# Reciprocal roots of the Hyena filters: a ScalarE square root and one Newton step in place of a bit trick and three, and the skip weight added on GpSimd

## The chip, the cores and the metric

The kernel runs on one core of one Trainium2 chip. The metric is the device time of one execution in microseconds (us), median of several runs. The profile names the engines PE (TensorE matmul), PEld (TensorE weight load), DVE (VectorE), ACT (ScalarE), POOL (GpSimd) and SP (the queue that issues most DMAs).

## What is computed

A trunk of two layers over 1024 latent tokens of width 1024, with a 256-token context. Layer 0 is neighbourhood attention beside a bidirectional gated DeltaNet. Layer 1 is an order-2 Hyena: its long convolutions take filters that a small network generates. The change is in those filters, which depend on no token:

```python
def hyena_filters(length, w1, b1, f1, w2, b2, f2, w3):
    ...
    hid = jnp.sin(f1 * (feats @ w1 + b1))
    hid = jnp.sin(f2 * (hid @ w2 + b2))
    h = (hid @ w3).astype(jnp.float32).reshape(length, HY_ORDER, HY_DIRS, HY_W)
    decay = jnp.abs(jnp.linspace(HY_DECAY_MIN, HY_DECAY_MAX, HY_W, dtype=jnp.float32))
    h = h * jnp.exp(-t * decay)[:, None, None, :]
    return h * lax.rsqrt(jnp.sum(h * h, axis=0, keepdims=True) + EPS)

def long_conv(u, h_fwd, h_bwd, skip):
    ...
    return (y_f + y_b + u32 * skip.astype(jnp.float32)).astype(u.dtype)
```

There are 2 orders x 2 directions x 1024 channels of filters, each of 1024 points. The skip weight is added to point 0 of the even part of a filter pair before its transform, which gives the same result as the last line.

## The kernel before

The program is written engine by engine in no order of its own: a scheduler in the build, which works with its own estimate of times, puts the instructions of each engine into one fixed list, and each engine works through its list in that order, waiting on semaphores. A change of a few instructions can therefore move others.

`start()` is the first stage. It does three things side by side. For each of eight blocks `cb` of 128 channels, `filter_pair` makes four filters (`od` = 0 to 3; two orders, two directions): two matmuls per half (tile `fh`), a multiply by the decay `dec` on DVE (L1265), a square with a row sum on ACT (L1267, into `ss`). After each second filter it adds EPS on DVE (L1270), takes the reciprocal root of the two sums (`rsqrt`, tile `rr`), and scales the two filters on ACT (L1273). `filter_block` then forms their sum `pp` (tile `fp`) on POOL (L1287) and difference on DVE (L1288), adds the skip weight to column 0 of `pp` (L1289), folds both (L1120 to L1143, L1301) and transposes them on PE; `filter_spectrum` multiplies by DFT matrices on PE and combines the results on DVE (L1324 to L1327) into the tile `G`, which goes to HBM for layer 1. The steps are staggered by `flush`: the block of one pair is put out while the next pair is made.

Beside this, `start()` brings in the latent tokens (`load_x`, `layer0_in`, L378 to L398), computes the modulation vectors (`mod_block`, L204 to L227) and the gate path of layer 0 (`zblock`, whose Tanh on ACT is L481 and whose product on DVE is L482). After `start()` comes `project()`, where PE runs the projections of layer 0.

`rsqrt` (L76 to L96) takes a first guess from the bits of its argument (L82, L83) and makes three Newton steps; for the two columns of a filter pair that is 12 DVE instructions, each on a 128x2 tile and each reading the one before it:

```python
for c in (3.0, 12.0, 768.0):
    nc.vector.tensor_tensor(t, s, s, ALU.mult)
    nc.vector.tensor_tensor(t, t, y, ALU.mult)
    ...
```

It is called 16 times for filters (tiles `fr_i`, `fr_t`, result `frr`); its other calls, for tokens and heads, have other tile names and do not change.

Of the kernel before, what the change touches and what calls it, by code (L numbers as in the profile page):

```python
# [10 lines left out]
F32 = mybir.dt.float32  # L11
# [3 lines left out]
AF = mybir.ActivationFunctionType  # L15
ALU = mybir.AluOpType
# [45 lines left out]
class Kernel:  # L62
# [13 lines left out]
    def rsqrt(self, out, y, n, pool, tag):  # L76

        nc = self.nc
        shape = [out.shape[0], n]
        ti = pool.tile(shape, I32, name=tag + "_i", tag="rsq_i")  # L80
        t = pool.tile(shape, F32, name=tag + "_t", tag="rsq_t")
        nc.vector.tensor_scalar(ti, y.bitcast(I32), 1, None, ALU.logical_shift_right)  # L82
        nc.vector.tensor_scalar(ti, ti, -1.0, float(0x5F3759DF), ALU.mult, ALU.add)  # L83

        s = ti.bitcast(F32)
        for c in (3.0, 12.0, 768.0):
            if n == 1:
                nc.vector.scalar_tensor_tensor(t, s, s, y, ALU.mult, ALU.mult)
            else:
                nc.vector.tensor_tensor(t, s, s, ALU.mult)  # L90
                nc.vector.tensor_tensor(t, t, y, ALU.mult)
            if c < 768.0:
                nc.vector.scalar_tensor_tensor(s, t, -c, s, ALU.add, ALU.mult)
            else:
                nc.vector.tensor_scalar(t, t, -c, -1.0 / 8192.0, ALU.add, ALU.mult)
                nc.vector.tensor_tensor(out, s, t, ALU.mult)  # L96

    def split(self, src, hi, lo, lo_eng=None, hi_eng=None):

        nc = self.nc  # L100
        if hi_eng is None:
            nc.scalar.copy(hi, src)  # L102
        else:
            hi_eng.tensor_copy(hi, src)
        (lo_eng or nc.gpsimd).tensor_tensor(lo, src, hi.bitcast(F32), ALU.subtract)  # L105
# [1136 lines left out]
    def filter_pair(self, cb, w3, fil, pst, psp, psf, fw):  # L1242

        nc, ap, fa = self.nc, self.ap, self.fa
        hid, trow, ndel, skip, mats = fil

        ws = fa.tile([P, 4, P], F32R, name=f"w3s_{cb}", tag="w3s", bufs=2)
        nc.scalar.copy(ws, w3)
        nc.gpsimd.tensor_tensor(w3[FFN:], w3[FFN:], ws[FFN:].bitcast(F32), ALU.subtract)
        nc.scalar.copy(ws[FFN:], w3[FFN:])  # L1250
        dec = fa.tile([P, L], F32, name=f"dec{cb}", tag="dec", bufs=1)
        nc.scalar.activation(dec, trow, AF.Exp, scale=ndel[:, cb:cb + 1])
        hh, hl = hid
        for od in range(4):
            if od % 2 == 0:
                ss = self.small.tile([P, 2], F32, name=f"fss{cb}_{od}", tag="fss")
                rr = self.small.tile([P, 2], F32, name=f"frr{cb}_{od}", tag="frr")
                hs = []
            t = fa.tile([P, 1028], F32, name=f"fh{cb}_{od}", tag="fh", bufs=4)
            for q in range(2):  # L1260
                sl = slice(q * 512, (q + 1) * 512)
                ps = psp.tile([P, 512], F32, name=f"fh{cb}_{od}_{q}", tag="g")
                nc.tensor.matmul(ps, ws[:, od, :], hh[:, sl], start=True, stop=False)
                nc.tensor.matmul(ps, ws[:FFN, od, :], hl[:, sl], start=False, stop=True)
                nc.vector.tensor_tensor(t[:, sl], ps, dec[:, sl], ALU.mult)  # L1265
            junk = self.xp.tile([P, L], BF16, name=f"fjk{cb}_{od}", tag="junk", bufs=1)
            nc.scalar.activation(junk, t[:, :L], AF.Square, accum_out=ss[:, od % 2:od % 2 + 1])  # L1267
            hs.append(t)
            if od % 2:
                nc.vector.tensor_scalar_add(ss, ss, EPS)  # L1270
                self.rsqrt(rr, ss, 2, self.small, f"fr{cb}_{od}")
                for d in range(2):
                    nc.scalar.activation(hs[d][:, :L], hs[d][:, :L], AF.Copy, scale=rr[:, d:d + 1])  # L1273
                self.flush(0, lambda a=(cb, od // 2, hs, skip, mats, pst, psf, fw): self.filter_block(*a))
# [7 lines left out]
    def filter_block(self, cb, o, hs, skip, mats, pst, psf, fw):  # L1282
        nc = self.nc
        nm = f"{cb}_{o}"
        pp = fw.tile([P, 1028], F32, name="fp" + nm, tag="fp", bufs=2)
        hf, hb = hs
        nc.gpsimd.tensor_tensor(pp[:, :L], hf[:, :L], hb[:, :L], ALU.add)  # L1287
        nc.vector.tensor_tensor(hb[:, :L], hf[:, :L], hb[:, :L], ALU.subtract)  # L1288
        nc.vector.tensor_tensor(pp[:, 0:1], pp[:, 0:1], skip[:, o, cb:cb + 1], ALU.add)  # L1289
        nc.gpsimd.memset(pp[:, L:L + 1], 0.0)  # L1290
        v, g = nc.vector, nc.gpsimd
        xTs = [None, None]
        for side, u in ((1, hb), (0, pp)):

            f = fw.tile([P, 10, P], F32, name=f"ff{nm}_{side}", tag="ff", bufs=2)
            f4 = f[:, 0:8, :].rearrange("p (h b k) m -> p h b k m", h=2, b=2)
            s1, d1, d2 = self.fold_tree(u, fw, f"ft{nm}_{side}", (g, v)[side])
            self.fold(f4[:, ::-1 if side else 1, :, 1, :], u, 1024, v, side)
            self.fold(f4[:, 0, :, 0, :], d1, 512, v, side)
            self.fold(f[:, 4, :], d2, 256, v, side)  # L1300
            g.tensor_tensor(f[:, 6:9:2, :], s1[:, 0:256].rearrange("p (a b) -> p a b", b=P),  # L1301
                            s1[:, 256:512].rearrange("p (a b) -> p a b", b=P), ALU.add)
            xTs[side] = self.transpose_all(f.rearrange("p a b -> p (a b)"), 9, fw, pst, f"fx{nm}_{side}", "xT", 3)
        self.flush(1, lambda: self.filter_spectrum(cb, o, xTs, mats, psf, fw))
# [619 lines left out]
```

## Time and profile before

| | us |
|---|---|
| median of 3 runs | 1977.28 |
| lowest and highest of them | 1976.55 and 1983.64 |
| the profiled execution, its time | 1978.44 |
| the same, span from first to last instruction | 1976.7 |
| PE busy | 1758.5 (89%) |
| DVE busy | 1452.9 (74%) |
| ACT busy | 817.4 (41%) |
| POOL busy | 709.7 (36%) |

The profiled execution took 1.7 us more than its span. Busy shares are averages over stages with different limits: the stage that the change touches, `start()`, fills about the first fifth of the span, and what matters is what each engine does in that stretch. A group's mean duration on DVE and POOL includes time in which an instruction stood waiting while it was already started. Lines are those of the kernel before.

### The profile page before, as it was taken

The page shows a single profiled execution, that of the slowest core. Times are in us where ns is not written, and L with a number is a line of the kernel's source. Part 1 is how long each engine was busy: PE and PEld are TensorE (multiplying, and loading weights), DVE is VectorE, ACT ScalarE, POOL GpSimd, SP SyncE. Part 2 cuts the span into 40 slices and gives each one's busy share as a digit, 9 for nine tenths or more (in the row PEclk, how much of TensorE's full clock was granted, in tenths as well). Part 3 has the DMA queues.
Part 4 walks back from the last instruction along what each step waited for, and adds up shares of the span by engine and source line. Part 5 has one row for each costly group of instructions (what it writes and reads, how often), then busy time and mean ns, then how long its engine had stood idle before and what let it go on. Part 6 is the DMA issues. An engine that isn't in the chain of part 4 may idle for free. (4 is left out here: it accounts for less than half of the span.)

```text
span 1976.7 us, 30354 instructions
## 1 busy us (share of the span) xinstructions
PE 1758.5 (89%) x11156; PEld 1425.0 (72%) x11156; DVE 1452.9 (74%) x2786; ACT 817.4 (41%) x1811; POOL 709.7 (36%) x878
## 2 busy tenths in 40 slices
PE   7698997999988989999977899879889899999888
PEld 2365765688866778787756787768778788878776
DVE  5999899666746644646554566579989999999766
ACT  4555574354534424233343344524323423433421
POOL 0776455422566777411253202511121221221310
PEclk9797998999998999999988999989999999999989
DMA  7423255423343564644688733511221121222324
GB/s 279 160 84 114 83 188 173 141 71 109 123 141 108 182 193 149 199 155 153 160 203 202 190 126 124 166 55 45 66 78 55 55 91 61 80 66 78 113 95 144
DMA packets 127471, 250.07 MB, mean 127 GB/s; under 512 B 43433, under 2 KB 65465, under 8 KB 125274
## 3 DMA queue, kind: packets, MB, share of 16 engines
q1 hardware_dynamic: 123482, 233.45, 36.0%
q0 software_dynamic: 3840, 14.68, 3.8%
q8 instruction: 88, 1.44, 0.3%
q14 instruction: 61, 0.50, 0.1%
HBM read 172.06 MB, written 76.03 MB: 126 GB/s over the span
## 5 line engine op out<-in xcount | busy, mean ns | idle before, releaser
L647 DVE SCALAR_TENSOR_TENSOR dacc<-dpad,convw,dacc 128x1024 f32<-128x1024 f32 (+1 forms) x80 | 84.4, 1084 | 24.1 <-ACT dacc L645 20.1
L116 PE MATMUL hx<-h1h,w1x_hi 128*128 128x512 f32 x256 | 101.1, 395 | 0.0
L116 PE MATMUL hx<-h1l,w1x_hi 128*128 128x512 f32 x256 | 101.0, 394 | 0.0
L116 PE MATMUL hx<-h1h,w1x_lo 128*128 128x512 f32 x256 | 100.7, 393 | 0.0
L112 PE MATMUL dn<-hh,wdn_lo 128*128 128x512 f32 (+1 forms) x256 | 94.9, 372 | 5.8 <-POOL wdn_lo L105 5.8
L111 PE MATMUL dn<-hl,wdn_hi 128*128 128x512 f32 (+1 forms) x256 | 94.8, 370 | 0.0
L110 PE MATMUL dn<-hh,wdn_hi 128*128 128x512 f32 (+1 forms) x256 | 94.5, 369 | 0.0
L750 POOL TENSOR_TENSOR sub<-Lb,Xb 80x31 f32<-80x31 f32 (+15 forms) x124 | 78.7, 635 | 38.8 <-DMA Lb<-lsc_d 18.3
L752 POOL TENSOR_TENSOR Xb<-Xb,sub 80x31 f32<-80x31 f32 (+15 forms) x124 | 84.9, 684 | 8.4
L105 POOL TENSOR_TENSOR w1x_lo<-w1x_raw,w1x_hi 128x1024 fp32r<-128x1024 f32 x16 | 53.7, 3355 | 90.6 <-ACT w1x_hi L102 90.5
L1045 ACT ACTIVATE pr<-pr,st 128x640 f32<-128x640 f32 (+1 forms) x64 | 51.3, 802 | 69.1 <-DVE st L1044 68.5
L112 PEld LDWEIGHTS dn<-hh,wdn_lo 128*128 128x128 f32 x256 | 48.7, 190 | 14.5 <-POOL wdn_lo L105 6.1
L1287 POOL TENSOR_TENSOR fp<-fh,fh 128x1024 f32<-128x1024 f32 x16 | 41.2, 2577 | 41.5 <-ACT fh L1273 41.5
L121 PE MATMUL pt<-ident,pr 128*128 128x128 f32 x304 | 48.6, 289 | 8.3 <-ACT pts L1058 4.2
L1616 DVE SCALAR_TENSOR_TENSOR hu<-hpx,hyconv,hu 128x1024 f32<-128x1024 f32 x32 | 53.5, 1671 | 2.1 <-ACT hu L1614 2.0
L1154 ACT COPY fx<-fx_ps 128x512 f32<-128x512 f32 (+1 forms) x96 | 43.8, 483 | 27.0 <-PE fx_ps L121 26.6
L116 PEld LDWEIGHTS hx<-h1h,w1x_lo 128*128 128x128 f32 x256 | 48.1, 188 | 9.1
L116 PEld LDWEIGHTS hx<-h1l,w1x_hi 128*128 128x128 f32 x256 | 48.1, 188 | 8.9
L116 PEld LDWEIGHTS hx<-h1h,w1x_hi 128*128 128x128 f32 x256 | 48.1, 188 | 8.9
L111 PEld LDWEIGHTS dn<-hl,wdn_hi 128*128 128x128 f32 x256 | 48.7, 190 | 8.0 <-issue 0.5
L1267 ACT ACTIVATE fjk<-fh 128x1024 bf16<-128x1024 f32 x32 | 33.9, 1059 | 49.5 <-DVE fh L1265 40.7
L110 PEld LDWEIGHTS dn<-hh,wdn_hi 128*128 128x128 f32 x256 | 48.7, 190 | 7.7
(565 smaller groups left out, 6069.5 us busy)
## 6 DMA issues: line engine op xcount, KB each, us to landing
hG<-g_d SPq DMA_DIRECT2D x16, 1088.0 KB
g_d<-G SPq DMA_DIRECT2D x16, 1024.0 KB
em_w<-in_em_w SPq DMA_DIRECT2D x24, 512.0 KB
om_w<-in_om_w SPq DMA_DIRECT2D x24, 512.0 KB
wz_raw<-in_w0z SPq DMA_DIRECT2D x16, 512.0 KB
w1x_raw<-in_w SPq DMA_DIRECT2D x16, 512.0 KB
wdn_raw<-in_w0dn SPq DMA_DIRECT2D x12, 512.0 KB
wn_raw<-in_w0na SPq DMA_DIRECT2D x12, 512.0 KB
```

The source lines that it names most:

```text
L105: (lo_eng or nc.gpsimd).tensor_tensor(lo, src, hi.bitcast(F32), ALU.subtract)
L110: nc.tensor.matmul(ps, wh, xh, start=start, stop=False)
L111: nc.tensor.matmul(ps, wh, xl, start=False, stop=False)
L112: nc.tensor.matmul(ps, wl, xh, start=False, stop=stop)
L116: ins = self.nc.tensor.matmul(*args, **kw)
L121: ins = self.nc.tensor.transpose(out, x, self.ident)
L647: nc.vector.scalar_tensor_tensor(acc[:, t0:t0 + n], pad[:, o + j:o + j + n], cw[:, blk, j:j + 1], acc[:, t0:t0 + n], ALU.mult, ALU.add)
L750: nc.gpsimd.tensor_tensor(tv, Lb[:, j + 1:, j:j + 1].broadcast_to([80, m, c]), Xb[:, j:j + 1, 0:c].broadcast_to([80, m, c]), ALU.mult)
L752: nc.gpsimd.tensor_tensor(Xb[:, j + 1:, 0:c], Xb[:, j + 1:, 0:c], tv, ALU.subtract)
L1045: nc.scalar.activation(pr[:, :n], pr[:, :n], AF.Exp, bias=st[:, 0:1], scale=-1.0, accum_out=st[:, 1:2])
L1154: nc.scalar.copy(out[:, j0:j0 + m, :].rearrange("p a b -> p (a b)"), ps[:, :m * P])
L1616: nc.vector.scalar_tensor_tensor(out[:, :L], pad[:, j:j + L], cw[:, blk, j:j + 1], out[:, :L], ALU.mult, ALU.add)
```

## The change

`rsqrt_root` is a new function, used for the filters alone. ACT takes the square root, DVE its reciprocal and one Newton step: one ACT and five DVE instructions on 128x2 tiles in place of twelve on DVE. The skip weight's add, one column of 128 rows, moves from DVE to POOL.

```diff
--- before.py
+++ after.py
@@ -94,6 +94,19 @@
             else:
                 nc.vector.tensor_scalar(t, t, -c, -1.0 / 8192.0, ALU.add, ALU.mult)
                 nc.vector.tensor_tensor(out, s, t, ALU.mult)
+
+    def rsqrt_root(self, out, y, n, pool, tag):
+
+        nc = self.nc
+        shape = [out.shape[0], n]
+        s = pool.tile(shape, F32, name=tag + "_s", tag="rsq_i")
+        t = pool.tile(shape, F32, name=tag + "_u", tag="rsq_t")
+        nc.scalar.activation(t, y, AF.Sqrt)
+        nc.vector.reciprocal(s, t)
+        nc.vector.tensor_tensor(t, s, s, ALU.mult)
+        nc.vector.tensor_tensor(t, t, y, ALU.mult)
+        nc.vector.tensor_scalar(t, t, -0.5, 1.5, ALU.mult, ALU.add)
+        nc.vector.tensor_tensor(out, s, t, ALU.mult)
 
     def split(self, src, hi, lo, lo_eng=None, hi_eng=None):
 
@@ -1268,7 +1281,7 @@
             hs.append(t)
             if od % 2:
                 nc.vector.tensor_scalar_add(ss, ss, EPS)
-                self.rsqrt(rr, ss, 2, self.small, f"fr{cb}_{od}")
+                self.rsqrt_root(rr, ss, 2, self.small, f"fr{cb}_{od}")
                 for d in range(2):
                     nc.scalar.activation(hs[d][:, :L], hs[d][:, :L], AF.Copy, scale=rr[:, d:d + 1])
                 self.flush(0, lambda a=(cb, od // 2, hs, skip, mats, pst, psf, fw): self.filter_block(*a))
@@ -1286,7 +1299,7 @@
         hf, hb = hs
         nc.gpsimd.tensor_tensor(pp[:, :L], hf[:, :L], hb[:, :L], ALU.add)
         nc.vector.tensor_tensor(hb[:, :L], hf[:, :L], hb[:, :L], ALU.subtract)
-        nc.vector.tensor_tensor(pp[:, 0:1], pp[:, 0:1], skip[:, o, cb:cb + 1], ALU.add)
+        nc.gpsimd.tensor_tensor(pp[:, 0:1], pp[:, 0:1], skip[:, o, cb:cb + 1], ALU.add)
         nc.gpsimd.memset(pp[:, L:L + 1], 0.0)
         v, g = nc.vector, nc.gpsimd
         xTs = [None, None]
```

In the changed kernel the lines after L97 are numbered 13 higher (L1270 is L1283, L1267 is L1280). The instruction counts of the two built programs differ so: DVE has 128 fewer (16 x 7 and 16), POOL 16 more, ACT 36 more: 16 square roots and 20 ACT_TABLE_LOAD. The list of ACT holds 7 such loads before and 27 after; 19 of the 20 stand among the filters (ten directly ahead of a root), one in the gates of `project()`. Behind the filters the lists of all engines are the same but for a few neighbours that change places.

DVE, around the reciprocal root of the second filter pair of block 2 (`fss` are the sums of squares, `fr` the root's work tiles, `frr` its result; `G` and `fh` belong to other filters in work). Before:

```order
L1270 TENSOR_SCALAR fss_2_1737<-fss_2_1737 128x2
L82 TENSOR_SCALAR fr_3_i<-fss_2_1737 128x2
L83 TENSOR_SCALAR fr_3_i<-fr_3_i 128x2
L90 TENSOR_TENSOR fr_3_t<-fr_3_i 128x2
L91 TENSOR_TENSOR fr_3_t<-fr_3_t,fss_2_1737 128x2
L1288 TENSOR_TENSOR fh_1_1605<-fh_0_1594,fh_1_1605 128x1024
L1289 TENSOR_TENSOR fp_0_1778<-fp_0_1778,skip 128x1
L93 SCALAR_TENSOR_TENSOR fr_3_i<-fr_3_t,fr_3_i 128x2
L1324 TENSOR_TENSOR G_0_1694<-fo_0_0_1724,fb_0_0_1713 128x2x128
L1325 TENSOR_TENSOR G_0_1694<-fo_0_0_1724,fb_0_0_1713 128x2x128
L1122 TENSOR_TENSOR ft_0_1_sd<-fh_1_1605 128x512
L1123 TENSOR_TENSOR ft_0_1_sd<-fh_1_1605 128x512
```

After:

```order
L1283 TENSOR_SCALAR fss_2_1707<-fss_2_1707 128x2
L1137 TENSOR_TENSOR ft_0_1_d_1749<-ft_0_1_sd 128x256
L105 RECIPROCAL fr_3_s<-fr_3_u 128x2
L106 TENSOR_TENSOR fr_3_u<-fr_3_s 128x2
L1278 TENSOR_TENSOR fh_0_1939<-fh_0_0_1940,dec_1935 128x512
L107 TENSOR_TENSOR fr_3_u<-fr_3_u,fss_2_1707 128x2
L1278 TENSOR_TENSOR fh_0_1939<-fh_0_1_1944,dec_1935 128x512
L393 TENSOR_SCALAR xss_1848<-xss_1848 128x2
L108 TENSOR_SCALAR fr_3_u<-fr_3_u 128x2
L82 TENSOR_SCALAR xrs_i<-xss_1848 128x2
L109 TENSOR_TENSOR frr_2_1708<-fr_3_s,fr_3_u 128x2
```

The thirteen small instructions from the add of EPS (L1270) to the result (L96), of which six stand here, reach over 34 rows of the list; the six that are left reach over 11. L105, the first behind ACT's root, stands two rows behind the add of EPS (L1283) that the root reads.

ACT, the same place: from the sum of squares of that pair's second filter onward. Before:

```order
L1267 ACTIVATE fjk_3_1759,fss_2_1737<-fh_3_1750 128x1024
L1252 ACTIVATE dec_1971<-trow,ndel 128x1024
L1154 COPY fx_1_1_1650<-fx_1_1_ps_1651 128x512
L1323 COPY fo_0_0_1724<-fb_0_0_1713 128x256
L1328 COPY G_0_1694<-fb_0_1_1696 128x256
L378 ACTIVATE xjk_1888,xss_1884<-x_8_1886 128x1024
L1250 CAST w3s_2265<-w_4_2263 64x512
L378 ACTIVATE xjk_1892,xss_1884<-x_9_1890 128x1024
L1154 COPY fx_1_1_1650<-fx_1_1_ps_1657 128x512
L1154 COPY fx_1_1_1650<-fx_1_1_ps_1663 128x128
```

After:

```order
L1280 ACTIVATE fjk_3_1729,fss_2_1707<-fh_3_1720 128x1024
L1265 ACTIVATE dec_1935<-trow,ndel 128x1024
L1263 CAST w3s_2217<-w_4_2215 64x512
L391 ACTIVATE xjk_1852,xss_1848<-x_8_1850 128x1024
L1341 COPY G_1_1517<-fb_1_0_1537 128x256
L1345 COPY G_1_1517<-fb_1_1554 128x128
L1167 COPY fx_1_1_1620<-fx_1_1_ps_1621 128x512
L104 ACT_TABLE_LOAD
L104 ACTIVATE fr_3_u<-fss_2_1707 128x2
L391 ACTIVATE xjk_1856,xss_1848<-x_9_1854 128x1024
```

The root (L104) stands eight rows behind the sum that it needs, with a table load directly ahead of it; the next gate Tanh (L494) brings another one.

POOL, at the first pairs of block 1 (`fp` is the pair's sum, `w3`, `hl` and `wz` are splits for other work). Before:

```order
L1287 TENSOR_TENSOR fp_0_1480<-fh_0_1296,fh_1_1307 128x1024
L1290 MEMSET fp_1_1633 128x1
L105 TENSOR_TENSOR hl_190<-xmod_7_530,hh_189 128x512
L1287 TENSOR_TENSOR fp_1_1633<-fh_2_1441,fh_3_1452 128x1024
L1122 TENSOR_TENSOR ft_0_0_sd<-fp_0_1480 128x512
L1123 TENSOR_TENSOR ft_0_0_sd<-fp_0_1480 128x512
L1301 TENSOR_TENSOR ff_0_1_1485<-ft_0_1_sd 128x2x128
```

After:

```order
L1300 TENSOR_TENSOR fp_0_1456<-fh_0_1284,fh_1_1295 128x1024
L1303 MEMSET fp_1_1603 128x1
L118 TENSOR_TENSOR hl_190<-xmod_4_503,hh_189 128x512
L1300 TENSOR_TENSOR fp_1_1603<-fh_2_1423,fh_3_1434 128x1024
L118 TENSOR_TENSOR hl_190<-xmod_5_512,hh_189 128x512
L1302 TENSOR_TENSOR fp_0_1456<-fp_0_1456,skip 128x1
L118 TENSOR_TENSOR wz_0_lo<-wz_0_raw,wz_0_hi 128x1024
L1314 TENSOR_TENSOR ff_0_1_1461<-ft_0_1_sd 128x2x128
L118 TENSOR_TENSOR hl_190<-xmod_6_521,hh_189 128x512
L1302 TENSOR_TENSOR fp_1_1603<-fp_1_1603,skip 128x1
L1135 TENSOR_TENSOR ft_0_0_sd<-fp_0_1456 128x512
```

The skip add (L1302) now stands ahead of the folds that read `fp` (L1135, and one on DVE), in one case with four rows between it and the sum (L1300) that it follows.

## Rows read from the trace of the kernel before

**Rows 1.** The page, its head and part 1: busy time of each engine, share of the span, instructions.

```profile
span 1976.7 us, 30354 instructions
...
PE 1758.5 (89%) x11156; PEld 1425.0 (72%) x11156; DVE 1452.9 (74%) x2786; ACT 817.4 (41%) x1811; POOL 709.7 (36%) x878
```

**Rows 2.** Busy time of each engine (and number of instructions) in six stretches of 50 us, with the granted clock of PE and the DMA traffic.

```profile
core 0: us, PE busy (x) PEld busy (x) DVE busy (x) ACT busy (x) POOL busy (x), PEclk, DMA share, GB/s
50.00:100.00 50.00, 33.78 (x196) 19.24 (x196) 44.19 (x83) 26.13 (x45) 36.51 (x35) 0.80 0.46 158
100.00:150.00 50.00, 45.18 (x239) 32.90 (x238) 48.60 (x96) 27.05 (x54) 36.69 (x34) 0.93 0.27 97
150.00:200.00 50.00, 41.03 (x159) 29.54 (x158) 48.06 (x95) 26.37 (x47) 30.31 (x30) 0.76 0.29 99
200.00:250.00 50.00, 45.87 (x251) 36.27 (x250) 44.76 (x93) 27.86 (x55) 24.14 (x30) 0.93 0.26 89
250.00:300.00 50.00, 46.65 (x299) 34.06 (x298) 47.38 (x128) 38.41 (x75) 26.58 (x35) 1.00 0.60 199
300.00:350.00 50.00, 38.52 (x273) 27.18 (x273) 46.83 (x100) 20.61 (x47) 29.08 (x32) 0.86 0.52 176
```

**Rows 3.** Groups of DVE instructions between 30 and 360 us: line, engine, operation, tiles, shape and count | busy us, mean ns of one | idle time of DVE before them and what ended it.

```profile
L1265 DVE TENSOR_TENSOR fh<-fh,dec 128x512 f32<-128x512 f32 x62 | 40.7, 679 | 3.9 <-PE fh L1264 3.9
L1143 DVE TENSOR_TENSOR ff<-ft_sd 128x256 f32<-128x256 f32 x32 | 32.1, 1013 | 0.0
L1288 DVE TENSOR_TENSOR fh<-fh,fh 128x1024 f32<-128x1024 f32 x16 | 22.3, 1392 | 0.5 <-POOL ft_d L1121 0.5
...
L91 DVE TENSOR_TENSOR fr_t<-fr_t,fss 128x2 f32<-128x2 f32 x48 | 14.6, 310 | 0.6
...
L90 DVE TENSOR_TENSOR fr_t<-fr_i 128x2 f32<-128x2 f32 x48 | 11.5, 245 | 0.5
...
L1289 DVE TENSOR_TENSOR fp<-fp,skip 128x1 f32<-128x1 f32 x16 | 10.0, 626 | 0.0
L93 DVE SCALAR_TENSOR_TENSOR fr_i<-fr_t,fr_i 128x2 f32<-128x2 f32 x32 | 9.8, 311 | 0.3
...
L82 DVE TENSOR_SCALAR fr_i<-fss 128x2 int32<-128x2 int32 x16 | 3.7, 233 | 0.0
L83 DVE TENSOR_SCALAR fr_i<-fr_i 128x2 int32<-128x2 int32 x16 | 3.6, 227 | 0.2
L96 DVE TENSOR_TENSOR frr<-fr_i,fr_t 128x2 f32<-128x2 f32 x16 | 3.1, 192 | 0.3
...
L95 DVE TENSOR_SCALAR fr_t<-fr_t 128x2 f32<-128x2 f32 x16 | 2.7, 167 | 0.3
```

**Rows 4.** DVE in order of time, at two places: start us, us, engine line operation tiles shape count.

```profile
156.09 0.16 DVE L1270 TENSOR_SCALAR fss<-fss 128x2 f32<-128x2 f32 x1
...
158.28 0.15 DVE L1289 TENSOR_TENSOR fp<-fp,skip 128x1 f32<-128x1 f32 x1
158.35 0.16 DVE L90 TENSOR_TENSOR fr_t<-fr_i 128x2 f32<-128x2 f32 x1
158.42 0.69 DVE L1122 TENSOR_TENSOR ft_sd<-fh 128x512 f32<-128x512 f32 x1
...
160.70 0.68 DVE L1265 TENSOR_TENSOR fh<-fh,dec 128x512 f32<-128x512 f32 x1
161.30 0.62 DVE L91 TENSOR_TENSOR fr_t<-fr_t,fss 128x2 f32<-128x2 f32 x1
...
294.14 0.16 DVE L93 SCALAR_TENSOR_TENSOR fr_i<-fr_t,fr_i 128x2 f32<-128x2 f32 x1
294.33 0.16 DVE L90 TENSOR_TENSOR fr_t<-fr_i 128x2 f32<-128x2 f32 x1
294.53 0.16 DVE L91 TENSOR_TENSOR fr_t<-fr_t,fss 128x2 f32<-128x2 f32 x1
```

**Rows 5.** POOL in order of time, at the first of those places.

```profile
158.58 1.65 POOL L1122 TENSOR_TENSOR ft_sd<-fp 128x512 f32<-128x512 f32 x1 [3.20 <-DVE fr_t L90]
160.19 1.72 POOL L1123 TENSOR_TENSOR ft_sd<-fp 128x512 f32<-128x512 f32 x1
```

**Rows 6.** ACT in order of time, near the start of the program: a small activation, and a table load with the activation behind it.

```profile
2.60 0.21 ACT L182 ACTIVATE c<-c 128x16 f32<-128x16 f32 x1 [0.58 <-DMA c<-in_cT]
...
12.04 1.28 ACT L1222 ACT_TABLE_LOAD   x1
13.34 0.63 ACT L1222 ACTIVATE hid<-hid 128x512 f32<-128x512 f32 x1
```

**Rows 7.** ACT in order of time: the end of a pair's second sum of squares.

```profile
152.58 0.19 ACT L1267 ACTIVATION_READ_ACCUMULATOR fjk<-fh 128x1 f32 x1
```

**Rows 8.** The nearest operations to those that the change brings: DVE's reciprocal of one column (min/median/max ns), POOL's fill of one column, POOL's smallest two-operand arithmetic (groups as in Rows 3).

```profile
L1046 DVE RECIPROCAL st<-st x64: 147/156/166, 984.2 to 1197.4; 128x1 f32<-128x1 f32 x64
...
L1290 POOL MEMSET fp<- 128x1 f32 x15 | 1.5, 99 | 10.2 <-DVE ff L1143 7.1 <-DVE fp L1289 3.2
...
L750 POOL TENSOR_TENSOR sub<-Lb,Xb 80x31 f32<-80x31 f32 x8 | 2.7, 342 | 30.7 <-DMA Lb<-lsc_d 18.3 <-DMA U<-xsc_d 12.1
```

**Rows 9.** Waits between 60 and 350 us: who waited for whom, us in total, times, longest.

```profile
DVE G L1324 <- ACT fo L1323: 0.6, 2, 0.5
...
ACT fjk L1267 <- DVE fh L1265: 40.7, 17, 5.6
```

## The prediction

> **What bounds the kernel now.** I start from the page: PE is busy 89% of the span, DVE 74% [rows 1]. That is an average over stages, so the second view is the busy time by stretches of 50 us in the stage that the change touches. From 50 to 350 us DVE is busy 279.8 of 300 us (the sum of six rows), PE 251.0, POOL 183.3, ACT 166.4 [rows 2]. PE's granted clock is 0.76 to 1.00 there, so part of its busy time is work at a lower clock, and PE could do this work in less; DVE could not. DVE is the bound of this stage, with some 20 us of idle time in 300. Behind it PE takes over, and whatever the stage ends earlier should move the rest of the program forward as it is, since the lists behind it are the same.
>
> The third view, the groups of DVE instructions, shows what the change takes hold of. The twelve instructions of the roots (L82 to L96 on `fr`) are busy 3.7 + 3.6 + 11.5 + 14.6 + 9.8 + 2.7 + 3.1 = 49.0 us for 192 instructions, and the skip add (L1289) 10.0 us for 16 [rows 3]. On two columns an instruction takes 0.16 us when nothing is in its way [rows 4]. At that price 208 of them would be 33.3 us and not 59.0: 25.7 us of their time is waiting. The timeline says for what: L91 at 161.30 took 0.62 us and ended at 161.92, just when POOL's addition of 160.19 ended (161.91), while L1265, which has one operand in PSUM, ran its usual 0.68 us beside the same POOL instruction [rows 4, 5]. A DVE instruction with two operands in SBUF stands still while POOL works on two operands of SBUF.
>
> **The change, part by part.** The profiled execution took 1978.44 us with a span of 1976.7; the sum is made against it, and it lies 1.2 us above the median of the runs.
>
> (a) *DVE has 128 instructions fewer: 16 x (12 - 5) and 16.* What one costs in a full list is the distance that it puts between its neighbours. With other work around it this is 0.07 us (158.28, 158.35, 158.42), in a bare chain, each waiting for the one before, 0.195 us (294.14, 294.33, 294.53) [rows 4]. Most of the chains are interleaved with other work, so I take 0.11: 128 x 0.11 = -14 us. Ends: 128 x 0.07 = -9 and 128 x 0.195 = -25. The reciprocal is a new operation in this stage, and at 0.156 us for one column [rows 8] it costs what the others do.
>
> (b) *Their waits for POOL.* Of the 25.7 us, the skip add has 10.0 - 16 x 0.16 = 7.4, and they go. The roots have 18.3. Nine instructions in twelve had two SBUF operands, three in five do now, so two thirds of it, 12.2, go as well. But 19.6 us isn't gained: where POOL is still at work, the next DVE instruction waits in the place of the one removed, unless it has an operand in PSUM. Of the three large groups shown, L1265 (40.7 us) has one, and L1143 and L1288 (32.1 and 22.3) do not [rows 3]; so some two fifths are gained: -8 us. Ends: 0 and -20.
>
> (c) *DVE now waits for ACT's root.* DVE adds EPS, ACT takes the root, DVE takes its reciprocal; whatever stands behind the reciprocal in DVE's list waits too: products with the decay (L1265), the folds, the parts of G, and through them PE. Two things cover the wait. DVE comes late to the sums: it added EPS at 156.09, when ACT had read the sum out at 152.77 [rows 4, 7]. And in most of the 16 places several large DVE instructions stand between the add and the reciprocal. They don't everywhere: in the place shown with the change one stands there, and ACT has six other instructions, a table load and the root to do behind the sum. A fully bare root costs a load and a small activation, 1.28 + 0.21 = 1.49 us [rows 6]; all 16 bare would be +24 us, none 0. I take four of them: +6.
>
> (d) *POOL adds the skip weight.* Between a one-column fill, 0.10 us, and the smallest two-operand arithmetic, 0.34 [rows 8], I take 0.2; 16 of them are 3 us on an engine that idles 117 of 300 us [rows 2]. In return POOL no longer waits for DVE's add. The fold on DVE that reads `fp` now waits for POOL's add, which may stand some POOL instructions behind. +1 us; ends 0 and, if each place bares one such POOL instruction of 1.7 us [rows 5] in four, +7.
>
> (e) *ACT has 20 table loads and 16 roots more.* 20 x 1.28 + 16 x 0.21 = 29 us [rows 6], on an engine that was busy 166 of 300 us and idled 40.7 us waiting for one product of DVE alone [rows 2, 9]. Most of it falls into such idle time. DVE waited only 0.6 us for ACT's copy `fo` [rows 9]; a load in front of such a copy or of the copies of transposes delays it by 1.28 us. I take two or three such delays that reach DVE: +3; ends 0 and +26, all loads bare.
>
> A table load took 1.28 us in this trace, and the activation behind it began 0.02 us after its end [rows 6]. The Trainium skill, "ScalarE: Activation LUTs", section "What ACT_TABLE_LOAD costs", counts a switch of sets at about 2.66 us, a drain added. By that the 20 loads would be an estimated 53 us of ACT's time, and (e) some +6; the trace shows no such drain, as far as its rows go.
>
> Sum: -14 - 8 + 6 + 1 + 3 = -12 us. 1978.44 - 12 = 1966.4 for a profiled execution, or 1965 beside the median of 1977.28.
>
> **The rivals.** *Slower: ACT's table becomes the path.* The root's set and the one of exp and tanh take turns, and each turn stands in ACT's list ahead of something that DVE or PE wants. If (c) and (e) are bare together, +24 + 26, less 11 for the ten loads that are counted in both, they outweigh (a) and (b): -22 + 39 + 1 = +18 us, 1995. It decides where more than about 15 of the 20 loads stand bare. Against it: ACT has 134 us of idle time in this stage [rows 2], and a load waits for nothing, so it can run while ACT would wait for the sum anyway. For it: the list puts ten loads directly ahead of roots. By the Trainium skill's figure ("ScalarE: Activation LUTs", "What ACT_TABLE_LOAD costs") eight bare loads would be enough.
>
> *No difference: the waits are handed on.* (b) gives nothing, since POOL's work is as long as before and DVE's large folds meet it anyway, and half the roots are bare: -14 + 12 + 1 + 3 = +2, with the small instructions at 0.07 rather +7, at 0.195 -9. About 1977. For it: L1143 has a mean of 1.01 us on 256 columns and L1122 took 0.69 on 512 [rows 3, 4], so large folds do wait for POOL already.
>
> *More than forecast: the waits go whole, and the roots are covered.* -14 - 15 + 2 = -27, 1950. For it: DVE's lateness of 3.3 us at 156.09 [rows 4, 7] is longer than a load and a root.
>
> **How the numbers follow.** Forecast 0.55 (1957 to 1972 by itself, half the distance of the ends of each term to either side, taken as independent), no difference 0.22, more 0.10, slower 0.13. 1965 is the forecast's. For 8 in 10 I go from 1949, which takes in the larger gain, to 1980, which takes in the case of no difference and leaves most of the slower one out. Half a per cent is 9.9 us, about what a measurement of this kernel can tell from no change. Of the forecast some eight tenths lie below 1967.4, with the larger gain 0.54 faster; the rest of it, the case of no difference and a small part of the slower one are 0.36 the same; 0.10 slower.
>
> **What would show it.** In the profile of the changed kernel: DVE's busy time between 50 and 350 us per finished filter falls, and its small instructions with it, from 59 us to some 20 (a, b); L1265, L1143 and L1288 keep their means or rise a little (what is handed on). Idle time of DVE ahead of the reciprocal, released by ACT's root, is near 6 us in all; above 15 us (c) is wrong. ACT shows 27 loads of 1.28 us with no gap behind them. The first projections of `project()` start some 12 us earlier than now, and the distance from there to the end stays. The prediction is wrong if DVE's waits for ACT and PE rise by more than its busy time falls, or if POOL's two-operand work takes DVE's time as before.

## The result: no faster, about half a per cent slower

The changed kernel took 1989.52 us in the median of its runs (1985.97 to 1997.32), the kernel before 1983.64 beside it (1976.52 to 1990.07). The ratio is 1.0046 with a 95% interval of 1.0027 to 1.0066; here and below the ratio is the one on record for the run, and it can differ from the quotient of the two medians (here 1.0030) by up to 0.2%. The forecast was 1965 us, in a range from 1949 to 1980; the time lies 9.5 us above the upper end. Some of that is the kernel before, which took 6.4 us more beside it than in the runs that the forecast started from; but a gain of 12 us was forecast, and there is a loss. One execution of all that follow, 2420.11 us of the kernel with idle roots, was in a slow state and is left out of its ratio.

### The profile page after: what moved, and what is told of

Read it like the earlier page. It is cut to its first block, busy times and chain, and to the rows that moved or that the text cites. A ratio compares the mean times of both kernels' runs of the same rounds, so it can differ in the third digit from the quotient of the medians.

```text
span 1989.7 us, 30241 instructions
## 1 busy us (share of the span) xinstructions
PE 1758.9 (88%) x11156; PEld 1426.4 (72%) x11156; DVE 1416.6 (71%) x2658; ACT 846.4 (43%) x1847; POOL 713.0 (36%) x894
## 5 line engine op out<-in xcount | busy, mean ns | idle before, releaser
L134 PE MATMUL fx_ps<-ident,ff 128*128 128x128 f32 x288 | 50.7, 300 | 15.7 <-ACT fx L1167 10.0
L134 PEld LDWEIGHTS fx_ps<-ident,ff 128*128 128x128 f32 x288 | 36.8, 152 | 30.6 <-ACT fx L1167 17.1
```

What stands on the lines that cost most here:

```text
L134: ins = self.nc.tensor.transpose(out, x, self.ident)
```

## The profile after

The page of the changed kernel, its head and part 1 (compare [rows 1]):

```profile
span 1989.7 us, 30241 instructions
PE 1758.9 (88%) x11156; PEld 1426.4 (72%) x11156; DVE 1416.6 (71%) x2658; ACT 846.4 (43%) x1847; POOL 713.0 (36%) x894
```

DVE works 36.3 us less than before, and the span is 13.0 us longer. The profiled execution took 1991.51 us. Where the time is lost is read from two instructions of PE, the first matmul of `ab` (the first use of all latent tokens, behind the filters) and the first of `dn` (the projections). The timeline of PE, before and then after; columns are start, duration, engine, line, operation, tiles:

```profile
379.40 0.47 PE L569 MATMUL ab<-hh,wab 128*32 128x512 f32 x1
389.81 0.40 PE L110 MATMUL dn<-hh,wdn_hi 128*128 128x512 f32 x1
```

```profile
391.49 0.48 PE L582 MATMUL ab<-hh,wab 128*32 128x512 f32 x1
401.94 0.40 PE L123 MATMUL dn<-hh,wdn_hi 128*128 128x512 f32 x1
```

Both come 12.1 us later. From `dn` to the end it is 1586.9 us before (1976.7 - 389.81) and 1587.8 after. So 12.1 of the 13.0 us lie in `start()`.

The stage from 40 us to that first `ab`, as one stretch, before and after (columns: length, then busy time and instructions of PE, PEld, DVE, ACT and POOL, PE's granted clock, DMA share, GB/s):

```profile
40.00:379.40 339.40, 287.28 (x1672) 203.99 (x1665) 309.62 (x677) 186.21 (x362) 192.71 (x201) 0.89 0.41 139
```

```profile
40.00:391.50 351.50, 286.52 (x1674) 204.10 (x1673) 284.27 (x550) 215.07 (x398) 201.22 (x221) 0.91 0.39 134
```

DVE is busy 25.3 us less (309.6 to 284.3). The time in which it isn't busy grows from 29.8 us (339.4 - 309.6) to 67.2. That is +37.4 - 25.3 = +12.1 us, the loss in the stage. PE's granted clock is a little higher after (0.91 against 0.89), so the clock isn't the cause.

The stretches of 50 us show where DVE idles (same columns, compare [rows 2]):

```profile
200.00:250.00 50.00, 47.23 (x260) 37.36 (x260) 39.04 (x71) 30.76 (x57) 28.77 (x34) 1.00 0.41 140
250.00:300.00 50.00, 38.44 (x254) 25.37 (x252) 34.86 (x80) 36.02 (x69) 23.79 (x29) 0.90 0.53 175
sum 300.00, PE 245.51 PEld 173.53 DVE 245.74 ACT 191.15 POOL 182.02; mean PE 40.92 PEld 28.92 DVE 40.96 ACT 31.86 POOL 30.34
```

DVE had 279.8 of 300 us before and has 245.7 now. The small instructions did what was expected of them. The groups of DVE and POOL from 30 to 372 us (instructions, total, mean in ns, then idle time ahead and what ended it; compare [rows 3]):

```profile
L1301 DVE TENSOR_TENSOR fh<-fh,fh 128x1024 f32<-128x1024 f32 x16 | 28.7, 1792 | 0.0
L107 DVE TENSOR_TENSOR fr_u<-fr_u,fss 128x2 f32<-128x2 f32 x16 | 5.6, 348 | 0.2
L106 DVE TENSOR_TENSOR fr_u<-fr_s 128x2 f32<-128x2 f32 x16 | 4.7, 295 | 0.2
L109 DVE TENSOR_TENSOR frr<-fr_s,fr_u 128x2 f32<-128x2 f32 x16 | 4.0, 249 | 0.3
L108 DVE TENSOR_SCALAR fr_u<-fr_u 128x2 f32<-128x2 f32 x16 | 3.6, 226 | 0.2
L105 DVE RECIPROCAL fr_s<-fr_u 128x2 f32<-128x2 f32 x16 | 2.5, 158 | 3.6 <-ACT fr_u L104 3.5
L1302 POOL TENSOR_TENSOR fp<-fp,skip 128x1 f32<-128x1 f32 x16 | 6.6, 414 | 0.4
```

The five take 20.4 us where 59.0 us stood before (the roots and the skip add), and the wait for ACT's root, which the forecast feared most, is 3.5 us in all. What DVE now waits for is elsewhere. Its longest waits before (40 to 379.4 us) and after (40 to 392 us) are these (total, times, longest; some rows are left out):

```profile
DVE G L1326 <- PE fb L116: 5.7, 3, 2.6
DVE G L1324 <- DMA g_d<-G: 4.4, 2, 2.7
...
DVE ff L1143 <- PE fx_ps L121: 2.4, 3, 1.5
```

```profile
DVE ff L1156 <- PE fx_ps L134: 15.0, 7, 5.7
DVE zt L495 <- ACT zt L494: 9.6, 3, 6.1
DVE G L1337 <- DMA g_d<-G: 8.3, 5, 5.4
DVE fss L1283 <- ACT fjk L1280: 5.4, 6, 1.3
DVE xmod L411 <- POOL hl L118: 4.7, 2, 4.0
DVE fr_s L105 <- ACT fr_u L104: 3.5, 5, 1.6
```

The wait for PE's transposes (`fx_ps`) grows from 2.4 to 15.0 us, the one for the DMA that takes `G` out from 4.4 to 8.3; before, `zt` for ACT, `xmod` for POOL and `fss` for ACT are not among the waits of 0.6 us and more. Neither the fold into `ff` nor the product `zt` nor the transfer of `G` is part of the change.

## The experiments

Two numbers are read from each profile: the start of the first `ab`, and DVE's busy time from 40 us to it. A profile is one execution, where the time is a median of several: the three profiles of the kernel before's lists in `start()` have `ab` at 379.4, 381.2 and 380.9 us. The ratio is to the kernel before on the same chip.

**Parts of the change, each with lists made anew.** *Skip add only*: the kernel before with one line changed.

```diff
-        nc.vector.tensor_tensor(pp[:, 0:1], pp[:, 0:1], skip[:, o, cb:cb + 1], ALU.add)
+        nc.gpsimd.tensor_tensor(pp[:, 0:1], pp[:, 0:1], skip[:, o, cb:cb + 1], ALU.add)
```

> The kernel before with the skip add moved to POOL, and nothing else. Theory L: faster by 1 to 6 us, 16 DVE instructions and their 10 us of busy time less (ratio 0.997 to 0.9995). Theory P: slower by 5 us or more, since folds on DVE and POOL now wait for an add that stands behind other work in POOL's list. Theory O: anywhere within 8 us, since the lists are made anew here too.

Measured: 1991.21 us, 1.0064 [1.0045, 1.0083].

*Root only*: the changed kernel with that line put back.

> The changed kernel with the skip add back on DVE: the root's change alone, with 22 more table loads than before. Theory L: slower than the kernel before by 8 to 18 us (ratio 1.004 to 1.009). Theory P: no slower than the kernel before, 0.995 to 1.000. Theory O: within 10 us of the changed kernel, either way.

Measured: 1977.06 us, 0.9978 [0.9960, 0.9997].

*No table loads*: the changed kernel with Copy for the square root. All lists are the same, only the 20 loads are gone; the filters' roots have wrong values.

```diff
-        nc.scalar.activation(t, y, AF.Sqrt)
+        nc.scalar.activation(t, y, AF.Copy)
```

> The changed kernel with a Copy in place of the Sqrt on ACT: the roots' values are wrong, the work is not. All engines' lists are the same as the changed kernel's, row by row, but for the 20 ACT_TABLE_LOAD, which are gone. Theory L (the loads are what the change costs: 20 x 1.28 us stand in ACT's list ahead of copies and gates that PE and DVE wait for): it is faster than the changed kernel by 20 us or more, and faster than the kernel before by 10 to 20 us (ratio 0.990 to 0.995), with DVE's waits for ACT's gate and for the transposes gone. Theory O (the new order of the lists costs it, whatever ACT's table does): within 5 us of the changed kernel, ratio 1.002 to 1.007. Theory P (POOL's skip add costs it): the same as theory O.

Measured: 1995.74 us, 1.0079 [1.0058, 1.0100], no faster than the changed kernel.

*One step only*: the kernel before, with one Newton step behind the bit trick, so that the roots are coarse. Nothing goes to ACT or POOL.

```diff
-                self.rsqrt(rr, ss, 2, self.small, f"fr{cb}_{od}")
+                self.rsqrt(rr, ss, 2, self.small, f"fr{cb}_{od}", (768.0,))
```

> The kernel before with one Newton step behind the bit trick, so the filters' roots are coarse: six DVE instructions for twelve, none on ACT, no table load, the skip add on DVE. What fewer DVE instructions bring by themselves. Theory L: faster than before by 8 to 15 us (96 instructions fewer at 0.11 us and some of their waits; ratio 0.992 to 0.996). Theory O: the gain of DVE's time does not reach the end of the stage, since its waits for PE grow with it: within 4 us of before.

Measured: 1979.13 us, 0.9999 [0.9984, 1.0014].

The loads are not what the changed kernel loses by: theory L fails in all four. The first two came out as theory P had them, and there theory O missed its bounds (10 us from the kernel before where it allowed 8, 12 us from the changed kernel where it allowed 10); the third, 6 us above the changed kernel, lies just outside both, and only the fourth is theory O's. In all four `start()` became longer: the first `ab` came at 397.9, 390.5, 395.3 and 387.1 us. The last one does strictly less work than the kernel before, 96 DVE instructions fewer and nothing in their place, and its stage is 6 to 8 us longer. That speaks for the lists, which the scheduler made anew in each of them but the third. So the skip add's 1.0064 need not be POOL's doing, but these four do not settle it; the next ones do.

**The order held.** The next kernels separate work from order. Edges of issue order, from each instruction to the one ahead of it on its engine, hold all five lists in a given order, without a semaphore or a wait of their own:

```python
for d in steps:          # the places of one engine's instructions, as differences
    at += d
    if last is not None:
        tc.add_manual_dep(mine[at], last.name, info, reason="pinned order")
    last = mine[at]
```

Holding by itself costs nothing that can be measured: the kernel before, held in its own order, took 0.9999 [0.9981, 1.0017] of its time (below). First the change and the old work, each in the other's order, then the two parts of the change in the order of before.

> The changed kernel, with every engine's list held in the order of the kernel before: its own instructions in the places of those they replace (ACT's root behind the row that stood ahead of the first step of the bit trick, the reciprocal at the latest step up to the eighth that the buffers allow, the last four of its five where the last four of the twelve stood, POOL's skip add directly behind the sum at L1287). Nothing is added but edges of issue order; PE and SP have the lists of before row for row. Theory O (what the change costs is the new order of the lists): with the order held the saved DVE time shows, start() ends 5 to 20 us earlier than in the kernel before (first matmul of ab at 360 to 375 us) and the time is 0.990 to 0.998 of before. Theory W (what costs is the work itself: the root's way over ACT and back, the add on POOL): as the changed kernel, 1.003 to 1.007, first ab at 388 to 396.

Measured: 1979.38 us, 1.0005 [0.9983, 1.0027], first `ab` at 374.7.

> The kernel before (twelve DVE instructions per root, skip add on DVE) with every engine's list held in the order of the changed kernel: PE and SP have the changed kernel's lists row for row; the first eight of the twelve stand where the reciprocal stood, the last four where the other four stood, the skip add where POOL's stood. Theory O: as slow as the changed kernel or slower, since it has the poor order and the old work: 1.005 to 1.015 of before, first ab at 390 to 410 us. Theory W: as the kernel before, 0.998 to 1.002, first ab at 376 to 384.

Measured: 2007.61 us, 1.0126 [1.0092, 1.0160], first `ab` at 414.8.

> The reciprocal root alone (skip add back on DVE) in the order of the kernel before. Theory O: most of the gain of both edits, 0.991 to 0.998 of before. Theory W with the root as the cost: 1.002 or more; with the skip add as the cost: as the same edit in its own order, 0.996 to 0.999, with start() longer than before as it was there (first ab near 390).

Measured: 1985.15 us, 1.0018 [0.9993, 1.0043], first `ab` at 384.1.

> The skip add on POOL alone, directly behind the sum at L1287, in the order of the kernel before. Theory O: within 0.3% of before (sixteen small DVE instructions gone, sixteen small POOL ones added), 0.997 to 1.002, first ab at 375 to 382 us. Theory W with POOL's add as the cost: as the same edit in its own order, 1.004 to 1.008, first ab at 390 to 400.

Measured: 1980.83 us, 1.0007 [0.9984, 1.0029], first `ab` at 383.4. In its own order the same edit took 1.0064.

| ratio to the kernel before | order of before | order of the changed kernel |
|---|---|---|
| old work | 0.9999 (held) | 1.0126 (held) |
| new work | 1.0005 (held) | 1.0046 |

So the order is the cause of the loss: by these ratios the old work in the new order is some 25 us slower than in the old one, and the new work in the old order is as fast as the kernel before, where in its own order it is 9 us slower. Theory P falls with the last run: POOL's add costs nothing that can be measured when the order is held. Half of theory O falls too: the gain it promised with the order held isn't in the times, and the root alone (1.0018) lies nearer to theory W, though its interval takes in 1. The work counts for more in the new order, where the new work is some 16 us faster than the old. The profile of the changed kernel held in the order of before, with `ab` at 374.7, is of its shortest execution (1974.45, the others up to 1989.22), so the few us that its stage is shorter say little.

What the new order does is seen best where the old work runs in it. DVE's waits of that kernel (the old work in the order of the changed kernel):

```profile
DVE ff L1143 <- PE fx_ps L121: 13.6, 7, 3.6
DVE G L1324 <- DMA g_d<-G: 10.8, 4, 5.6
DVE zt L482 <- ACT zt L481: 6.2, 2, 4.7
DVE fss L1270 <- ACT fjk L1267: 4.5, 5, 1.3
...
DVE xmod L398 <- POOL hl L105: 3.2, 2, 2.6
```

They are the waits that grew in the changed kernel, with the twelve instructions of the bit trick back in place; none of them needs the new root. One place shows how they arise. In the new list of DVE the product `zt` stands directly behind the last step of a root. In ACT's list the Tanh that it needs stands eight rows behind the first scaling that waits for the same root (DVE's rows, then ACT's):

```
365 L109 TENSOR_TENSOR frr_0_2510<-fr_1_s,fr_1_u 128x2
366 L495 SCALAR_TENSOR_TENSOR zt_0_894<-zt_0_894,z_0_869 128x512

226 L1286 ACTIVATE fh_0_2511<-fh_0_2511,frr_0_2510 128x1024
227 L1286 ACTIVATE fh_1_2522<-fh_1_2522,frr_0_2510 128x1024
...
233 L494 ACT_TABLE_LOAD
234 L494 ACTIVATE zt_0_894<-z_0_869 128x512
```

The timelines of DVE and ACT there, in the changed kernel:

```profile
247.84 1.18 DVE L109 TENSOR_TENSOR frr<-fr_s,fr_u 128x2 f32<-128x2 f32 x1
255.11 0.69 DVE L495 SCALAR_TENSOR_TENSOR zt<-zt,z 128x512 f32<-128x512 f32 x1 [6.08 <-ACT zt L494]
```

```profile
249.06 2.19 ACT L1286 ACTIVATE fh<-fh,frr 128x1024 f32<-128x1024 f32 x2 [1.42 <-DVE frr L109]
253.19 1.28 ACT L494 ACT_TABLE_LOAD   x1
254.48 0.60 ACT L494 ACTIVATE zt<-z 128x512 f32<-128x512 f32 x1
```

And on DVE with the old work in the same order:

```profile
266.58 1.18 DVE L96 TENSOR_TENSOR frr<-fr_i,fr_t 128x2 f32<-128x2 f32 x1
272.43 0.69 DVE L482 SCALAR_TENSOR_TENSOR zt<-zt,z 128x512 f32<-128x512 f32 x1 [4.67 <-ACT zt L481]
```

DVE ends the root at 249.02 and then stands for 6.08 us, since everything behind `zt` in its list must wait with it. The old work stands there for 4.67 us; the difference, 1.41, is about the one table load (1.28) that the old work does not have at this place. In the order of before five other small instructions stood between the end of a root and this `zt`, and none of the eight early products `zt` waited.

**The lists behind `start()`.** The kernels above differed in one more thing. From the first `dn` to the end, root only and one step took 1572.6 and 1575.0 us, all others so far 1581 to 1592. Their lists behind the stage differ too: between the orders of before and of root only, some 290 of 11,900 instructions there stand in another place, 30 of them transfers of SP.

> The changed kernel with the lists of start() held in the order of the kernel before, and behind it every engine's list in the order that the root alone (in its own order) had. In that run, and in the one-step run, the part from the first matmul of dn to the end took 1573 and 1575 us, in the others 1581 to 1592. Theory R (this difference is the order of the lists behind start()): the part behind takes 1572 to 1577 us here, and the time is 0.990 to 0.995 of before, which beats both kernels. Theory V (it is a difference from one execution to the next): 0.998 to 1.002, as the changed kernel held in the order of before throughout.

Measured: 1966.91 us, 0.9922 [0.9893, 0.9952]; 1578.3 us from `dn` to the end, just above theory R's 1572 to 1577.

> The kernel before, its work and start() unchanged, with the lists behind start() in the order that the root alone had. Theory R: the part behind start() takes 1572 to 1577 us, the time is 0.991 to 0.996 of before. Theory V: 0.999 to 1.001 in time, the part behind 1580 to 1592.

Measured: 1967.05 us, 0.9926 [0.9899, 0.9953]; 1574.0 us from `dn` to the end.

The control for both is the kernel before, held in its own order.

> The kernel before, each list held in its own order: the same program on every engine. Both theories: 0.999 to 1.001 of before. It shows what holding costs by itself, and gives a second profile of the same lists: with theory R the part behind start() takes 1584 to 1590 us again, with theory V anything from 1572 to 1592.

Measured: 1981.09 us, 0.9999 [0.9981, 1.0017]; first `ab` at 381.2, 1586.5 us from `dn` to the end.

Theory R holds, but for that 1.3 us: in eight profiles with the lists of root only behind `start()` (its own, the two above and the five below) this part takes 1571.9 to 1578.3 us, in five with the lists of before 1586.1 to 1591.7. The kernel before is beaten by 14 us with no instruction changed, and the changed kernel in that order beats both as well. Between the two the change itself makes no difference that these intervals (some 6 us to either side) could show. Which of the moved rows does it was not tried.

**What eats the saving when the order is held.**

> The changed kernel held in the order of the kernel before, with the lists behind start() that the root alone had (the version that beat both kernels), and Copy in place of the square root on ACT: all lists are the same, only the 22 table loads that the roots bring in this order are gone (22 x 1.28 = 28 us of ACT). The filters' roots have wrong values here. With the loads the first matmul of ab came at 374.6 us, DVE stood idle 37.4 us until then against 30.2 us with the old work in the same order, and DVE and PE waited for ACT more often. Theory A (in a good order the loads keep the saved DVE time from reaching the end of start()): first ab at 362 to 371 us, DVE idle below 33 us, and the time 0.986 to 0.990 of before. Theory N (the loads cost nothing here either, the saved time ends in the hand-over between PE and DVE): first ab at 373 to 376 us, 0.990 to 0.994 of before.

Measured: 1957.62 us, 0.9882 [0.9857, 0.9906]; first `ab` at 373.3, DVE idle 37.9 us until then. The time is theory A's, the stage and DVE's idle time are not, so neither theory is settled by it. The next four ran on one chip; the idle instructions are one line behind the add of EPS, with Sqrt or with Copy.

```diff
                 nc.vector.tensor_scalar_add(ss, ss, EPS)
+                nc.scalar.activation(rr, ss, AF.Sqrt)
```

> The kernel before with the better lists behind start(), all lists as there, plus sixteen idle square roots on ACT (of the same sums, written to the tile that DVE overwrites with its own result later), at the places where the changed kernel's roots stand when it is held in this order: they bring 22 table loads, 28 us of ACT, and right values. Theory A (loads cost in a good order): 3 to 8 us slower than the same kernel with idle copies, the stage up to the first matmul of ab longer by 2 to 8 us. Theory N: within 2 us of it, first ab at 380 to 382 us in both.

Measured: 1974.25 us (1973.60 without the execution of 2420.11), 0.9972 [0.9957, 0.9986]; first `ab` at 387.2.

> The same with idle copies in place of the idle roots: the same lists without the 22 loads. Both theories: 0.992 to 0.994 of before, as without the idle instructions, first ab at 380 to 382 us. It is the base of the kernel with the idle roots.

Measured: 1970.21 us, 0.9947 [0.9928, 0.9967], a little slower than expected; first `ab` at 379.6.

> The version that beat both kernels (changed kernel, order of before in start(), other lists behind it), a second time, beside the one without loads: 0.990 to 0.994 of before, first ab at 374 to 375 us. Theory A: 5 us or more slower than the one without loads. Theory N: within 3 us of it.

Measured: 1966.01 us, 0.9926 [0.9908, 0.9943]; first `ab` at 380.2, later than expected.

> The same without the 22 loads (Copy in place of the square root, so the filters' roots have wrong values), a second time and on the same chip: Theory A: 0.986 to 0.990 of before; Theory N: 0.990 to 0.993. In both the first ab at 372 to 374 us.

Measured: 1957.77 us, 0.9884 [0.9864, 0.9905]; first `ab` at 372.9.

The stage up to the first `ab` in these four, in the same order (the columns of the stretches above):

```profile
40.00:387.20 347.20, 290.70 (x1657) 207.10 (x1655) 311.89 (x666) 213.53 (x396) 188.54 (x201) 0.86 0.39 135
```

```profile
40.00:379.60 339.60, 285.65 (x1669) 203.10 (x1661) 311.34 (x677) 188.03 (x378) 190.59 (x201) 0.90 0.41 138
```

```profile
40.00:380.20 340.20, 287.60 (x1672) 204.87 (x1672) 299.40 (x549) 214.63 (x399) 198.79 (x217) 0.90 0.41 138
```

```profile
40.00:372.90 332.90, 285.86 (x1673) 203.56 (x1674) 293.31 (x552) 188.29 (x378) 201.94 (x217) 0.90 0.41 141
```

Theory A holds in the times: with the loads the kernel takes 3.4 us more with the old work (1973.60 against 1970.21) and 8.2 us more with the new (1966.01 against 1957.77). In the second pair no execution with loads (1962.11 to 1968.20) is as short as one without (1955.49 to 1960.26), and the first runs of the same two kernels say the same (0.9922 against 0.9882). ACT is busy some 26 us more in both pairs. In these four profiles the loads make the stage 7.6 us longer with the old work (387.2 against 379.6) and 7.3 us with the new (380.2 against 372.9), but what they cost in the stage is less sure than that. Two other profiles of the new work with loads in this order had `ab` at 374.6 and 374.7, less than 2 us behind those without, and in the first pair PE's granted clock differs as well (0.86 against 0.90). The idle roots compute right values, so the values aren't the reason. PE's waits show where the loads arrive. In the second pair, with loads and then without:

```profile
PE fb L129 <- ACT G L1341: 4.9, 5, 1.9
PE fx_ps L134 <- ACT fx L1167: 4.1, 7, 1.4
```

```profile
PE fx_ps L134 <- ACT fx L1167: 1.7, 6, 0.4
```

PE waits for ACT's copies of `G` and `fx`; without the loads the first of these waits falls from 4.9 to 0.6 us and the second from 4.1 to 1.7. In the changed kernel's own order DVE idles 67 us anyway, and there the loads cost nothing that could be measured.

## Why the prediction was wrong

*The step that failed* is the one from "DVE is the bound of this stage" to the sum: DVE's saved time, (a) and (b) with -22 us, was taken as the time by which `start()` ends earlier, as if inside the stage the new lists would serve the new work as well as the old ones had served the old. The text had counted rows in the lists and looked at a few places of them, but it has no term for the lists themselves: the waits of DVE for PE's transposes, for the gate's Tanh, for the transfer of `G` and for the sums of squares stand in the sum at nothing. In the new order these and others hold DVE up for 37.4 us more, against 25.3 us that its work became shorter; with the order held the loss is gone (1.0005), and the new order alone costs the old work 1.26%. The step behind it, that the end of the stage moves "the rest of the program" as it is, held: 1586.9 us before and 1587.8 after, only later and not earlier.

*The sum by itself* failed too: with the order held there is no gain of 12 us. Its terms against the order held (row (e) from the four runs on one chip):

| term | forecast | measured with the order held |
|---|---|---|
| (a) + (b) DVE's time | -22 | DVE's busy time 309.6 to 296.9: -12.7 (310.5 in a second profile of before: -13.6) |
| (c) wait for the root | +6 | 4.0 (L105, order of before), 2.4 with the better lists behind `start()` |
| (d) skip add on POOL | +1 | 1.0007 [0.9984, 1.0029] for that edit alone |
| (e) table loads | +3 | +3.4 and +8.2 in time, +7.6 and +7.3 in the stage of these profiles, under 2 in others |
| all | -12 | 1.0005 [0.9983, 1.0027] |

The stage of the changed kernel in the order of before (columns as above):

```profile
40.00:374.70 334.70, 282.02 (x1672) 201.13 (x1665) 296.86 (x549) 214.38 (x399) 197.90 (x217) 0.92 0.41 141
```

(b) was too large: with (a) at its -14, next to nothing is left of its -8. The waits for POOL were handed on to the large instructions more than the three fifths assumed, as two groups of DVE show (30 to 360 us), before and then with the order of before held:

```profile
L1143 DVE TENSOR_TENSOR ff<-fh 128x512 f32<-128x512 f32 x16 | 20.4, 1278 | 0.4 <-PE fx_ps L121 0.4
```

```profile
L1301 DVE TENSOR_TENSOR fh<-fh,fh 128x1024 f32<-128x1024 f32 x16 | 26.7, 1666 | 0.0
L1156 DVE TENSOR_TENSOR ff<-fh 128x512 f32<-128x512 f32 x16 | 25.3, 1580 | 1.1 <-PE fx_ps L134 1.1
```

L1288 (now L1301) took 22.3 us for the same work before [rows 3], so these two took over 4.4 and 4.9 us; the second profile of the old lists had 24.3 and 21.8 us, so part of it is spread. This is the mechanism of the rival "the waits are handed on", and with the order held that rival's time is the one that came. That is in part luck: it had 12 us for (c), where some 4 came, and 3 us for (e), where up to 8.2 came. In its own order the changed kernel's DVE was busy 25.3 us less, near the -22, but it stood idle instead.

(c) and (d) were right in kind and near in size. The wait for the root with the order of before held:

```profile
DVE fr_s L105 <- ACT fr_u L104: 4.0, 5, 1.6
```

(e) was right in its mechanism and too small: 3 us, against 3.4 and 8.2 in time. The rival that made ACT's table the path priced (c) and (e) together at 39 us, where the two come to 12 at most (4.0 of wait and 8.2 of time, in which loads ahead of roots may count twice); and in the changed kernel's own order, where that rival's 1995 us lie near the measured time, the loads cost nothing that could be measured, so its mechanism is not what came. In its price the ten loads counted twice are 12.8 us at 1.28 each, not 11. By the Trainium skill, "ScalarE: Activation LUTs", section "What ACT_TABLE_LOAD costs", a switch is 2.66 us with a drain, an estimated 53 us for 20 of them. The trace does not agree: the load at 253.19 ends at 254.47, and the Tanh starts at 254.48.

*What was right*: the small instructions' 59 to some 20 us (20.4), the wait for the root near 6 us (3.5), 27 loads, and the distance from the stage to the end. The sign that was named as the one that would make the forecast wrong, that DVE's waits for ACT and PE rise by more than its busy time falls, is what came: they rise from 20.5 to 52.3 us (waits of 0.3 us and more, until the first `ab`), +31.8 against -25.3.

*What stays open*: why this order, and not another, came out of the build; and which of the moved rows behind `start()` bring the 14 us. Without loads the saved work is worth 12.4 us of time (1957.77 against 1970.21) where the stage is 6.7 us shorter (372.9 against 379.6); that is no contradiction, since the profiles are of the longest execution of the one (1960.26) and the shortest of the other (1965.86), 5.6 us apart.

## What to carry to other kernels

Where a scheduler writes the lists, an edit has two effects, its work and a new order, and in a tuned kernel the second can be larger than the first: here the new order cost 8 us with the new work and 25 with the old, where the new work in the old order made no difference that could be measured (8 to 12 us of gain without its table loads). Hold the order while you measure an edit, and afterwards measure the orders by themselves; one of them was worth 14 us with no work changed. A saving on the busiest engine counts only as far as the engine that it leans on (here ACT with its table loads) has the time when it is asked.

## What the runs showed of the hardware

A load of ACT's table took 1.28 us in every trace here, and 20 to 22 of them cost the kernel's time between nothing that could be measured (in the changed kernel's own order) and 8.2 us (in the order of before). Edges of issue order cost nothing that could be measured (0.9999 [0.9981, 1.0017]). Beside POOL's work on SBUF a small DVE instruction with two SBUF operands still stands: L109, on two columns, took 1.18 us from 247.84 to 249.02 where 0.16 is usual, and POOL's addition beside it in the changed kernel ended then:

```profile
247.74 1.28 POOL L1136 TENSOR_TENSOR ft_sd<-fp 128x512 f32<-128x512 f32 x1
```

The old L96 took 1.18 us at the same place of the list, with the old work in the new order.
